# RWKV-7 diagonal-block inverse: forward substitution by columns in place of rows

## The chip, the core and the metric

The kernel runs on one core of a Trainium2 chip. The metric is device time in microseconds (us) of one execution. It was run three times before the change; the median is 3178.09 us. Engine names in the rows: PE is TensorE (PEld its weight loads), DVE is VectorE, ACT is ScalarE, POOL is GpSimd, SP is SyncE, which here only issues DMAs. A name with a q (SPq, ACTq) is the engine's queue of DMA issues, waits and the like.

## The reference, cut to what matters

Two layers of a streaming-encoder trunk are computed on 1024 tokens of width 1024. Layer 0 has RWKV-7 time mixing beside a Mamba-2 scan; then come cross-attention and an MLP; layer 1 has an mLSTM in place of the pair. The change is in the RWKV-7 part, whose core is this recurrence over time:

```python
def rwkv7_scan(r, w, k, v, a, b):
    def step(S, inp):
        r_t, w_t, k_t, v_t, a_t, b_t = inp
        sa = jnp.einsum('bhvk,bhk->bhv', S, a_t)
        S = S * w_t[:, :, None, :] + sa[..., None] * b_t[:, :, None, :] + v_t[..., None] * k_t[:, :, None, :]
        return S, jnp.einsum('bhvk,bhk->bhv', S, r_t)
    ...
```

The kernel computes it in 16 chunks of 64 tokens for 8 heads. Inside a chunk the dependence of later tokens on earlier ones is a unit lower triangular system, so the kernel needs, for each chunk and head, the inverse T of I - A, where A is strictly triangular and 64 x 64. It inverts the two 32 x 32 diagonal blocks by forward substitution on VectorE and joins them with small matmuls later (lines 663 to 678).

## The kernel before, in words

The program is written as one main thread of large matmuls and many generators ("streams"). The planner keeps `self.pt`, an estimate of TensorE's time, which `mm` and `tr` raise with each matmul (lines 193 to 205). A generator that yields a number asks to be resumed when `pt` has grown by that number times `self.lag` (line 163; the lag is 1.8 in this stage, 3.0 from line 1073 on); one that yields a function waits for a condition. `tick` after each group of matmuls resumes what is due; `until` jumps `pt` forward when the main thread has nothing to do. The order of the trace is the priority; a scheduler then puts each engine's instructions into a fixed order. On the chip each engine runs its own in order.

Layer 0's mixer (`mixer0`, line 959) runs these parts:
- The main thread projects the normalised input with 26 weight tiles (`fm`, 48 matmuls of 128x512 each). Each weight tile is loaded on the ACT queue (line 231) and split in two parts, a cast on ACT (line 217) and a subtraction on VectorE (line 218).
- `rw_pair(p)` (line 495) prepares head pair p, for p 0 to 3. At its end four groups (lines 569 to 588, 2.5 planned us apart) multiply `bk` and `va`, mask the result into the tile `AB` (line 578) and store it on SP (line 579), and store transposed copies `tm` (lines 587, 588). Earlier it takes the product of line 564, and the tile `u` for `newton` (lines 487 to 493, 523).
- `rw_inverse(q)` (line 591) handles head pairs 2q and 2q+1, once both are prepared. It loads the diagonal blocks of all 16 chunks, 2 heads and 2 pairs into `As`, one 32 x 32 block per partition (128 of them), and makes `Ts` from the identity. Row i of `Ts` is then the sum over k of A[k, i] times row k, with `pr` holding the products. At the end `As` gets the transpose of `Ts` and twelve DMAs store both (line 626, eight on SP and four on ACT).
- `pr`, `AB` and `u` share one ring of two tiles of the pool `tmp` (tag "tmp", line 973).
- The last weight tiles are those of `z` (`mb_z`, line 818: a copy, a sigmoid of line 824 and a product on GpSimd of line 825) and, before the last of them, of dt (`mb_dt`, line 797: a chain of small operations over ACT and VectorE that ends in the scan of line 815).
- After the last projection the main thread waits for both inverses (line 1069), closes the pools of the stage, and goes on with the memory side of layer 1 (`memside`). The chunk loop (`rw_chunk`, line 630) waits for the inverses at line 652, loads T (lines 654, 655) and runs the recurrence; the Mamba windows (`mb_window`, line 828) load `a8` at line 845. Both are streams beside `memside`.

GpSimd runs the products of lines 548, 554, 788 and 825 during this stage.

Of the kernel before, what the change touches and what calls it, by code (L numbers as in the profile page):

```python
# [14 lines left out]
ALU = mybir.AluOpType  # L15

P = 128
# [38 lines left out]
class Trunk:  # L56
# [534 lines left out]
    def rw_inverse(self, q, pool, pt, S):  # L591


        nc = self.nc
        yield lambda: 0.0 if self.rw_done[0] >= 2 * q + 2 else None
        B = 32
        block = lambda s: self.ed.tile([P, B, B], F32, name=self.n(s), tag="xo") if q else pool.tile([P, B, B], F32, name=self.n(s), tag=s)
        As = block("As")
        for a in range(2):
            for j in range(2):  # L600
                src = S["ABK"][:, CH * j:CH * j + CH, 2 * q + a, j, :]
                r0 = 64 * a + 32 * j
                for b in range(2):
                    v = src[:, B * b:B * b + B, B * b:B * b + B]
                    self.ld1(As[r0 + 16 * b:r0 + 16 * b + 16], v)
        Ts = block("Ts")
        yield 9.0
        nc.gpsimd.memset(Ts[:], 0.0)
        nc.gpsimd.memset(Ts[:].rearrange("p i k -> p (i k)")[:, 0:B * B:B + 1], 1.0)
        for i in range(1, B):  # L610

            if i < 8 and i % 4 == 1 or i >= 8:
                pr = pt.tile([P, B, B], F32, name=self.n("pr"), tag="tmp")
            pv = pr[:, :i, :i]
            nc.vector.tensor_tensor(pv, Ts[:, :i, :i].rearrange("p k j -> p j k"), As[:, :i, i].unsqueeze(1).broadcast_to([P, i, i]), ALU.mult)  # L615
            nc.vector.tensor_reduce(Ts[:, i, :i], pv, mybir.AxisListType.X, ALU.add)  # L616
            if i >= 7 or i % 4 == 0:
                yield 0.4 + 0.0025 * i * i
        nc.vector.tensor_copy(As[:], Ts[:].rearrange("p i k -> p k i"))
        for n_, x in enumerate((Ts, As)):  # L620
            for a in range(2):
                for j in range(2):
                    r0 = 64 * a + 32 * j
                    for b in range(n_ + 1):
                        dst = S["T"][n_, :, CH * j + B * b:CH * j + B * b + B, 2 * q + a, B * b:B * b + B]
                        (nc.scalar if b else nc.sync).dma_start(dst, x[r0 + 16 * b:r0 + 16 * b + 16])
        self.inv_done[0] += 1
        self.inv_t = self.pt + 5.0
# [1220 lines left out]
```

## Time and profile before

| | |
|---|---|
| three runs | 3170.97, 3178.09, 3180.80 us; median 3178.09 |
| profiled execution | 3178.65 us, of which the span of the trace is 3176.9 us |
| mean granted TensorE clock | 0.969 of full speed |
| busy: TensorE / VectorE / ACT / GpSimd | 2957.1 / 1793.5 / 1316.6 / 621.2 us |
| line 615 (multiply), 62 instructions | 62.48 us of VectorE |
| line 616 (reduction), 62 instructions | 31.02 us of VectorE |
| first inverse | 333.95 us to about 452 us |
| second inverse | 472.45 us to about 533 us |

Times of a row are counted from the start of the span. A row of a timeline gives start, duration (for a merged row, of all of it), engine, line, operation, output from inputs, shapes, and in brackets how long the engine had been idle before and what released it. Busy times can overlap between engines; a matmul's end is modelled. Instructions of one engine can overlap a little.

### The profile page before, as it was taken

Reading aid. Unit: us, or ns where it says so; the run is one execution under the profiler, and the core shown is the slowest. Engines: PE = TensorE matmul, PEld = TensorE weight load, DVE = VectorE, ACT = ScalarE, POOL = GpSimd, SP = SyncE. Lnnn points to the kernel's source line nnn. Section 1 sums busy time; section 2 is a strip of 40 time slices with the busy share of each in tenths; the row PEclk is TensorE's granted clock in tenths of the full one; section 3 lists DMA queues with packets and bytes.
Section 4 is the critical chain, followed back from the end, with each engine's and each line's share of the span. In section 5 each row is a group of like instructions: output and inputs, shape, how many; then the busy total and the mean of one; then the engine's idle time right before and its main releaser. Section 6 shows DMA issues by size and latency. Waiting matters only on the chain.

```text
span 3176.9 us, 40016 instructions
## 1 busy us (share of the span) xinstructions
PE 2957.1 (93%) x15652; PEld 2394.3 (75%) x15652; DVE 1793.5 (56%) x2283; ACT 1316.6 (41%) x2096; POOL 621.2 (20%) x632
## 2 busy tenths in 40 slices
PE   8999997889889989998999999899999899989998
PEld 8777676867677867776788778777788677768877
DVE  7345788655653465664656732145644656646566
ACT  6546533434333343444443433133343444444433
POOL 1111121022221123333001110011221233330002
PEclk9999999979999989999999999999999999999999
DMA  7734466668552123445744543446331234457456
GB/s 262 262 93 124 121 165 167 211 223 273 177 180 99 67 91 128 138 137 205 257 157 159 177 146 99 123 128 227 114 113 67 80 134 141 136 193 259 144 163 221
DMA packets 274493, 505.21 MB, mean 159 GB/s; under 512 B 57328, under 2 KB 160176, under 8 KB 274304
## 3 DMA queue, kind: packets, MB, share of 16 engines
q1 hardware_dynamic: 220608, 317.50, 31.2%
q0 software_dynamic: 26144, 99.69, 8.8%
q10 hardware_dynamic: 27552, 85.47, 8.3%
q8 instruction: 123, 2.02, 0.3%
q14 instruction: 66, 0.54, 0.1%
HBM read 347.66 MB, written 154.89 MB: 158 GB/s over the span
## 4 chain that ended last, share of the span: by engine, by line
PE 66%; DVE 12%; DMA 11%; issue 4%; ACT 3%; SPq 1%; POOL 1%; DVEq 0%; ACTq 0%; POOLq 0%
PE pd L201 38%; PE pm L201 22%; PE ph L201 4%; DMA rw<-in_ff_dn_dram 3%; PE pm L205 3%; DVE wb L218 2%; DVE pr L615 2%; DMA ru<-scr 1%; DVE Ts L616 1%; DVE sx L218 1%; DMA scr<-mo 1%; DVE T L218 1%; DVE ce L786 1%; DMA yr<-scr 1%; DMA wr<-in_ev_w_out_dram 1%
## 5 line engine op out<-in xcount | busy, mean ns | idle before, releaser
L201 PE MATMUL pd<-xth,wb 128*128 128x512 f32 x1120 | 364.9, 401 | 11.1 <-DVE wb L218 10.9
L218 DVE TENSOR_TENSOR wb<-wr,wb 128x1024 fp32r<-128x1024 f32 (+1 forms) x148 | 180.9, 1228 | 273.1 <-ACT wb L217 272.6
L201 PE MATMUL pd<-w,sh 128*128 128x512 f32 x1024 | 324.5, 398 | 8.8 <-DVE y L341 5.6
L201 PEld LDWEIGHTS pd<-xth,wb 128*128 128x128 f32 x1120 | 210.9, 190 | 67.3 <-DVE wb L218 13.6
L201 PE MATMUL pd<-T,wb 128*128 128x512 f32 x1008 | 251.0, 395 | 11.3 <-DVE wb L218 5.8
L201 PEld LDWEIGHTS pd<-T,wb 128*128 128x128 f32 x1008 | 191.3, 190 | 55.1 <-DVE wb L218 6.7
L217 ACT ACTIVATE wb<-wr 128x1024 fp32r<-128x1024 f32 (+1 forms) x148 | 154.6, 1050 | 187.0 <-PE pm L201 116.3
L201 PEld LDWEIGHTS pd<-w,sh 128*128 128x128 f32 x1024 | 192.0, 190 | 51.5 <-ACT w L217 5.8
L201 PE MATMUL pd<-xtl,wb 128*128 128x512 f32 (+1 forms) x576 | 229.1, 399 | 0.0
L201 PE MATMUL pd<-xb,wb 128*128 128x512 f32 x768 | 194.3, 403 | 28.0 <-DVE ub L1564 20.4
L201 PE MATMUL pd<-w,sl 128*128 128x512 f32 x512 | 203.2, 397 | 0.0
L201 PEld LDWEIGHTS pd<-xb,wb 128*128 128x128 f32 x768 | 143.1, 190 | 73.4 <-DVE ub L1564 30.5
L201 PE MATMUL pm<-wb,xth 128*128 128x512 f32 x512 | 163.1, 399 | 0.5 <-DVE G L1213 0.5
L201 PE MATMUL pm<-wb,wb 128*128 128x512 f32 x672 | 157.1, 389 | 0.0
L201 PE MATMUL pm<-T,wb 128*128 128x512 f32 x528 | 140.4, 410 | 10.9 <-DVE T L218 5.2
L201 PEld LDWEIGHTS pm<-wb,wb 128*128 128x128 f32 x672 | 126.1, 188 | 26.1
L218 DVE TENSOR_TENSOR wb<-ws,wb 128x1024 fp32r<-128x1024 f32 x64 | 90.9, 1420 | 94.0 <-ACT wb L217 94.0
L201 PEld LDWEIGHTS pm<-T,wb 128*128 128x128 f32 x528 | 104.9, 200 | 37.3 <-DVE T L218 6.7
L217 ACT ACTIVATE wb<-ws 128x1024 fp32r<-128x1024 f32 x64 | 67.6, 1057 | 147.3 <-PE pd L201 122.4
L201 PEld LDWEIGHTS pd<-xtl,wb 128*128 128x128 f32 (+1 forms) x576 | 107.7, 187 | 25.8 <-issue 2.6
L201 PE MATMUL pd<-wb,wb 128*128 128x512 f32 x480 | 113.8, 394 | 5.1 <-DVE wb L218 5.1
L201 PE MATMUL pm<-sx,sx 128*128 128x512 f32 x384 | 96.3, 406 | 21.9 <-ACT sx L217 21.3
(436 smaller groups left out, 6309.4 us busy)
## 6 DMA issues: line engine op xcount, KB each, us to landing
scr<-ub POOLq DMA_DIRECT2D x32, 1792.0 KB, 8.6
ru<-scr SPq DMA_DIRECT2D x112, 512.0 KB
rw<-in_ff_dn_dram SPq DMA_DIRECT2D x82, 512.0 KB
scr<-xo POOLq DMA_DIRECT2D x39, 512.0 KB, 3.0
scr<-mo POOLq DMA_DIRECT2D x32, 512.0 KB, 5.6
xo<-scr SPq DMA_DIRECT2D x32, 512.0 KB
wr<-in_ff_upT_dram SPq DMA_DIRECT2D x32, 512.0 KB
wf<-in_ff_upT_dram SPq DMA_DIRECT2D x32, 512.0 KB
```

The lines of the kernel that those rows point to most:

```text
L201: self.nc.tensor.matmul(out, lhsT=lhsT, rhs=rhs, start=start, stop=stop, skip_group_check=on)
L205: self.nc.tensor.transpose(out, in_, self.ident if ident is None else ident)
L217: self.nc.scalar.activation(hi, src, AF.Copy)
L218: self.nc.vector.tensor_tensor(lo, src, hi.bitcast(F32), ALU.subtract)
L615: nc.vector.tensor_tensor(pv, Ts[:, :i, :i].rearrange("p k j -> p j k"), As[:, :i, i].unsqueeze(1).broadcast_to([P, i, i]), ALU.mult)
L616: nc.vector.tensor_reduce(Ts[:, i, :i], pv, mybir.AxisListType.X, ALU.add)
L786: nc.vector.scalar_tensor_tensor(e[:, d:], sg[:, :T - d], col(3 - d), e[:, d:], ALU.mult, ALU.add)
```

## The change

Row-wise substitution is replaced by column-wise substitution in the loop of `rw_inverse`. Once row k of `Ts` is final, its products with A[k, i] are added into all rows i below it: a multiplication over n x m elements and an addition of the same size in place, with n = 31 - k rows and m = k + 1 columns. The reduction is gone. The products lie contiguous at the head of `pr`. A `pr` tile is taken every eighth step. The stream yields after every second step, with a due time that grows with n x m.

```diff
-        for i in range(1, B):
-
-            if i < 8 and i % 4 == 1 or i >= 8:
+        for k in range(B - 1):
+
+            if k % 8 == 0:
                 pr = pt.tile([P, B, B], F32, name=self.n("pr"), tag="tmp")
-            pv = pr[:, :i, :i]
-            nc.vector.tensor_tensor(pv, Ts[:, :i, :i].rearrange("p k j -> p j k"), As[:, :i, i].unsqueeze(1).broadcast_to([P, i, i]), ALU.mult)
-            nc.vector.tensor_reduce(Ts[:, i, :i], pv, mybir.AxisListType.X, ALU.add)
-            if i >= 7 or i % 4 == 0:
-                yield 0.4 + 0.0025 * i * i
+            n, m = B - 1 - k, k + 1
+            pv = pr[:].rearrange("p i k -> p (i k)")[:, 0:n * m].rearrange("p (i j) -> p i j", j=m)
+            nc.vector.tensor_tensor(pv, As[:, k, m:].unsqueeze(2).broadcast_to([P, n, m]), Ts[:, k, :m].unsqueeze(1).broadcast_to([P, n, m]), ALU.mult)
+            nc.vector.tensor_tensor(Ts[:, m:, :m], Ts[:, m:, :m], pv, ALU.add)
+            if k % 2:
+                yield 0.4 + 0.004 * n * m
         nc.vector.tensor_copy(As[:], Ts[:].rearrange("p i k -> p k i"))
```

## Rows read from the trace of the kernel before

**Rows 1.** The page, chain that ended last: shares by engine, then by line.
```profile
PE 66%; DVE 12%; DMA 11%; issue 4%; ACT 3%; SPq 1%; POOL 1%; DVEq 0%; ACTq 0%; POOLq 0%
PE pd L201 38%; PE pm L201 22%; PE ph L201 4%; DMA rw<-in_ff_dn_dram 3%; PE pm L205 3%; DVE wb L218 2%; DVE pr L615 2%; DMA ru<-scr 1%; DVE Ts L616 1%; DVE sx L218 1%; DMA scr<-mo 1%; DVE T L218 1%; DVE ce L786 1%; DMA yr<-scr 1%; DMA wr<-in_ev_w_out_dram 1%
```
**Rows 2.** Stretches: length; PE, PEld, DVE, ACT, POOL busy; granted clock; DMA.
```profile
333.00:460.00 127.00, 115.48 (x599) 83.74 (x599) 106.05 (x121) 57.99 (x75) 22.95 (x16) 0.97 0.47 129
460.00:500.00 40.00, 38.43 (x184) 30.45 (x180) 28.78 (x50) 10.74 (x15) 10.27 (x5) 1.00 0.91 275
500.00:560.00 60.00, 40.42 (x206) 34.02 (x207) 43.75 (x35) 18.44 (x19) 6.18 (x4) 0.86 0.53 131
560.00:900.00 340.00, 299.04 (x3240) 252.84 (x3240) 199.24 (x377) 142.89 (x318) 69.92 (x85) 0.90 0.64 213
```
**Rows 3.** Timeline of PE, 388 to 565 us, rows with idle time before them.
```profile
427.74 1.06 PE L205 MATMUL pm<-ct,bk 64*128 64x64 f32 x8 [1.93 <-DVE xn L564]
...
441.51 0.73 PE L205 MATMUL pm<-ct,bk 64*128 64x64 f32 x8 [1.12 <-ACT tm L587]
453.21 0.46 PE L205 MATMUL pm<-ct,bk 64*128 64x64 f32 x4 [1.60 <-ACT tm L587]
501.54 0.50 PE L201 MATMUL pd<-xth,wb 128*128 128x512 f32 x1 [3.00 <-DVE wb L218]
516.29 1.15 PE L201 MATMUL pd<-xth,wb 128*128 128x512 f32 x2 [5.07 <-DVE wb L218]
534.09 0.58 PE L201 MATMUL ph<-mh,wb 128*128 128x256 f32 x1 [5.49 <-ACT zs L824]
...
559.43 0.38 PE L205 MATMUL pm<-ct,a 8*128 8x8 f32 x2 [7.07 <-DMA a<-scr]
```
**Rows 4.** Timeline of DVE: one step of either size, stretched ones, weight splits.
```profile
333.95 1.62 DVE L615 TENSOR_TENSOR pr<-Ts,As 128x1 f32<-128x1 f32 x1 [1.14 <-DMA As<-scr]
...
472.45 0.16 DVE L615 TENSOR_TENSOR pr<-Ts,As 128x1 f32<-128x1 f32 x1 [4.58 <-DMA As<-scr]
...
500.79 0.69 DVE L218 TENSOR_TENSOR wb<-wr,wb 128x512 fp32r<-128x512 f32 x1
...
504.02 3.42 DVE L615 TENSOR_TENSOR pr<-Ts,As 128x576 f32<-128x576 f32 x1
...
515.02 1.22 DVE L218 TENSOR_TENSOR wb<-wr,wb 128x1024 fp32r<-128x1024 f32 x1
...
527.73 1.86 DVE L615 TENSOR_TENSOR pr<-Ts,As 128x961 f32<-128x961 f32 x1
...
531.85 1.13 DVE L616 TENSOR_REDUCE Ts<-pr 128x31 f32<-128x961 f32 x1
```
**Rows 5.** Line 744: durations ns min/median/max, first and last start, shapes.
```profile
L744 DVE TENSOR_TENSOR yw<-yw,st x8: 681/691/693, 601.6 to 843.8; 128x512 f32<-128x512 f32 x8
```
**Rows 6.** Stretches, tile pr alone (lines 615, 616): length; DVE busy; clock; DMA.
```profile
390.00:452.00 62.00, 29.84 (x24) 1.00 0.46 130
472.00:534.00 62.00, 47.04 (x62) 0.94 0.54 171
```
**Rows 7.** Timeline of POOL: the product beside the multiply at 504.02.
```profile
503.99 2.37 POOL L825 TENSOR_TENSOR ze<-ze,zs 128x1024 f32<-128x1024 f32 x1 [0.77 <-ACT zs L824]
```
**Rows 8.** Timeline of ACT: the casts of the two late weight tiles.
```profile
492.50 0.64 ACT L217 ACTIVATE wb<-wr 128x512 fp32r<-128x512 f32 x1
...
503.79 1.06 ACT L217 ACTIVATE wb<-wr 128x1024 fp32r<-128x1024 f32 x1
```
**Rows 9.** Timelines of DVE and of SP's queue: dt scan, load of a.
```profile
534.82 4.20 DVE L815 TENSOR_TENSOR_SCAN ce<-rm,cs 8x1024 f32<-8x1024 f32 x1 [0.20 <-DMA scr<-ce]
...
551.04 1.84 SPq L845 DMA_DIRECT2D a<-scr  x1
```
**Rows 10.** Chain that ended last, in order of time: a store of AB.
```profile
324.85 4.69 DMA scr<-AB
```

## The prediction

> **What bounds the kernel now.** I read the chain of work that ended last first: TensorE holds 66% of it, and VectorE comes next with 12% [rows 1]; the two lines of the substitution stand in that list by name on the page. So VectorE can matter, but only in stages. The busy times by stretch show where: from 333 to 460 us, where the first inverse runs, VectorE is busy 106 of 127 us; from 500 to 560 us, where the second one ends, TensorE falls to 40.42 of 60 us, and its mean granted clock to 0.86 [rows 2]. Third, TensorE's idle times and what ended them [rows 3]: 3.00 and 5.07 us wait for the weight split of line 218 (VectorE), 5.49 us for the last sigmoid (ACT, line 824), 7.07 us for a small load; the earlier three (4.65 us in all) wait for VectorE's line 564 and for ACT's line 587. Fourth, VectorE's order of time [rows 4, 8]: the split that began at 500.79 had its ACT half done at 493.14 (492.50 + 0.64), the one at 515.02 at 504.85. For 8 and 10 us they stood behind steps 19 to 27 of the second substitution. What ends last in this stage is VectorE's queue, with TensorE (in order) behind it.
>
> **What is removed and added on VectorE.** Row by row, step i multiplies i x i elements and sums them by a reduction: the sum of i² for 1 to 31 is 10,416 elements in each of the two instructions. By columns, step k multiplies n x m and adds n x m, n = 31 - k, m = k + 1: the sum is 5,456, so 10,912 elements in two instructions against 20,832. Instructions stay 62 an inverse. Rates: the multiply reads both inputs at steps of 32 elements; 961 elements took 1.86 us, one element 0.16 [rows 4], so 1.77 ns an element. The reduction of 961 took 1.13 us; with the same start that is 1.01 ns. For the new multiply (one input repeated along the innermost index, the other contiguous) the nearest row is line 744, an addition with such a repeated input: 512 elements in 0.691 us [rows 5], so 1.04 ns; the contiguous 128x1024 of line 218 took 1.22 us [rows 4], the same rate. The bounds for the new pair are 1.04 and 1.77 ns; I take 1.04, since both new instructions walk contiguous rows and the repeated input has a row of its own. Only the first step's addition, with rows of one element, walks at a step of 32, and it has 31 elements.
>
> Old, undisturbed: 62 x 0.16 + 10,416 x (1.77 + 1.01) ns = 9.9 + 29.0 = 38.9 us an inverse. New: 9.9 + 10,912 x 1.04 ns = 9.9 + 11.3 = 21.2 us (29.2 at the other bound). The pauses between a step's dependent instructions are as many as before.
>
> **What GpSimd does to them.** The multiply at 504.02 took 3.42 us where its neighbours' rate gives 1.18, and GpSimd's line 825 ran from 503.99 for 2.37 us [rows 4, 7]. Of the 62 multiplies eight are stretched like this (the first at 333.95, the last at 504.02 [rows 4]). So the second inverse was busy 47.04 us [rows 6] and not 38.9: 8.1 us are such stretches. No reduction was stretched so, and the change puts two-input additions in the place of all 62. I still take what I find in the old one, cut to 5 us, since the new inverse lasts less long; bounds 0 and 8 and, if each addition that meets such a GpSimd instruction is held too, some 3 more (it would have met the next multiply anyway). Sum: 47 to 26 us, 21 us off VectorE in each inverse. The Trainium skill, "GPSIMD Engine Reference", section "Key points", says that GpSimd shares its SBUF interfaces with VectorE, with contention for VectorE instructions that have two SBUF inputs: it speaks against the additions and agrees with the row of 3.42 us; if it doubled the old loss of 8 us, the second inverse would be busy 37 us and save 10 in place of 21.
>
> The Trainium skill, "VectorE: DVE Perf Modes", section "Rules for kernel authors", calls the reduction "the slowest DVE op". Were the multiply no dearer than it, the old inverse would be 31.0 us and the saving undisturbed 10 in place of 18; here the reduction is the cheaper of the two by rows 4, and the measurement decides.
>
> **Where in the inverse it is saved.** Old costs grow with i², new ones are largest in the middle and equal at both ends. The first twelve steps get dearer: 24 x 0.16 + 650 x 2.78 ns = 5.6 us before, 24 x 0.16 + 1,846 x 2.08 ns = 7.7 us after. The last twelve fall from 3.8 + 7,946 x 2.78 ns = 25.9 to 7.7 us. Those last twelve are what stood before the two weight splits.
>
> **The order.** The planner is told 0.4 + 0.0025 i² at 26 places, 36.3 us, now 0.4 + 0.004 nm at 15 places, 16.9 us; with the lag of 1.8 these are 65 and 30 us of planned TensorE time. So the second inverse, which outlived the projections, is planned to end inside them. It issues twelve stores (eight SP, four ACT); they move from behind the dt scan and the last z into the projections, past the z stores on SP and the weight casts on ACT. They cost nothing while a projection's matmuls cover them; without that cover, up to 1.84 us an issue, as that of a [rows 9], 7 us for ACT's four. The chunk loop's first matmuls, which wait for the inverse's loads, may then stand in TensorE's order among the last projections. Nothing before shows such a wait; the nearest row is the 7.07 us for a load [rows 3], so it costs 0 to 7; I take 2, as matmuls are put late where their inputs are planned late. The pr tile is now taken 4 times an inverse in place of 26, each held for eight steps in the ring of two that AB and u also use; I take 0, and give its price below.
>
> **What of it reaches the end**, by TensorE's idle times:
> - 333 to 460 us: of the 4.65 us of waits [rows 3] I take 3. VectorE spends 29.84 us on the substitution between 390 and 452 [rows 6], after the change under 10; the head gets dearer, so not all.
> - 501 and 516 us: of 8.07 us 7, and 3 us of clock. The granted clock has two levels, 1.2 and 2.4 GHz; a mean of 0.86 over 60 us [rows 2] means some 17 us at the lower level, so at most 8 us of lost work, in this stretch behind idle times. It was 1.00 in the 40 us before.
> - 534 us: of 5.49 us 2. The last z's cast and sigmoid stand on ACT behind the dt chain, which waits for VectorE; two table loads remain.
> - 559 us: of 7.07 us 5. The load of a (issued 551.04) follows the dt scan on VectorE (534.82, 4.20 us) [rows 9], which comes some 15 us earlier, while TensorE arrives 12 to 15 us earlier.
> - against it the new wait, 2.
> Sum 3 + 10 + 2 + 5 - 2 = 18 us. What is late next: TensorE itself with the projections, then the loads of the chunk loop. From 560 to 900 us TensorE is busy 299 of 340 us [rows 2] and moves as a whole. The profiled execution took 3178.65 us (span 3176.9), 0.6 us over the median of 3178.09; 3178.65 - 18 = 3160.7, against the median 3160. Bounds of the sum: all waits and the clock away and no new wait, 4.65 + 8.07 + 8 + 5.49 + 7.07 = 33, with some 5 more from a reordered stage behind: 3140. Only half of 501 and 516 and the new wait in full: 4 + 0 + 0 - 7, about no gain.
>
> **Rivals.**
> (1) VectorE comes free and another wait takes the place: the dt chain over ACT with its table loads, SP's queue, or the chunk loads. For it: the waits at 534 and 559 us name ACT and a DMA, not VectorE [rows 3]. Against: the two at 501 and 516 name VectorE alone. The gain is then 2 to 8 us: 3170 to 3176, say 3173.
> (2) Slower: the ring of two. AB's slot is held from its two masks (128x512 like line 744's, 2 x 0.69 us [rows 5]) until its store has landed; one such store stands in the chain with 4.69 us [rows 10]. That is 6.1 us, against a planned 2.5 x 1.8 = 4.5 between groups. While one pr holds the other slot through eight steps, each group is 1.6 us late, eight groups of two pairs make 13 us; a u tile in the one free slot, for four instructions of 128x1024 at 1.22 us [rows 4] in each pair, adds 10, and the lower clock after such stops some 5. That is 28 us, and with 15 gained elsewhere 3192. It decides from the point at which groups have only one slot for their whole length. Against: the old form took slots 26 times and TensorE's waits name no slot; the first inverse becomes shorter.
> (3) It doesn't do what it says: the repeated input doesn't stream, and both instructions run at 1.77 ns. Then 8 us less are saved in each inverse, the waits of 501 and 516 shrink by half and the gain is about 8: 3170.
> (4) More than forecast: the chunk recurrence starts inside the projections and the stage behind loses waits too: 33 to 38 us, 3143.
>
> **Chances.** Forecast (10 to 30 us off) 0.62; (1) 0.16; (2) 0.12; (3) 0.04; (4) 0.06. A difference of 0.3%, 9.5 us, is about what a measurement of this kernel can tell from none. Faster: 0.62 + 0.06 = 0.68; the same: 0.16 + 0.04 = 0.20; slower 0.12. The range leaves out (2) and the edge of (1) and (4): 3140 to 3177.
>
> **What would show it.** The two lines' busy time per inverse near 26 us against 47; a middle step of 256 elements at 0.43 us for both instructions; last step short. TensorE's idle times for line 218 near 500 us gone, and the clock of that stretch near 1.00; the scan of line 815 some 15 us earlier; memory-side matmuls starting some 15 us before 534. Wrong would be: new idle times of TensorE for cT or cTT loads, or for AB slots (line 578) in the stretch from 333 to 460 us, or a stage from 560 to 900 us that grows by what was won before it.

## The result, and the profile after

The changed kernel took 3139.68 us, the median of 5 runs (3134.78 to 3144.98), against 3178.09 us before. The ratio is 0.9881 with a 95% interval of 0.9867 to 0.9895, so the change gains 38 us, or 1.2%. The forecast was 3160 us with a range of 3140 to 3177: the direction was right, the gain was twice as large, and the time lies just below the range.

The profiled execution after the change took 3139.83 us (span 3138.1 us). Line numbers from 613 on are higher by one than before: the multiply is L616, the addition L617.

First the stretches of the two inverses, VectorE's work on the tile pr alone (length; VectorE busy; granted clock; DMA), to set against rows 6:

```profile
338.00:418.00 80.00, 29.32 (x62) 0.96 0.45 123
458.00:500.00 42.00, 30.42 (x62) 1.00 0.68 224
```

The second inverse is busy 30.42 us where it was 47.04 [rows 6]. VectorE's timeline shows the middle step, one stretched addition and the dt scan:

```profile
483.17 0.42 DVE L616 TENSOR_TENSOR pr<-As,Ts 128x256 f32<-128x256 f32 x1
483.63 0.42 DVE L617 TENSOR_TENSOR Ts<-Ts,pr 128x256 f32<-128x256 f32 x1
...
491.40 3.15 DVE L617 TENSOR_TENSOR Ts<-Ts,pr 128x175 f32<-128x175 f32 x1
...
520.79 2.28 DVE L816 TENSOR_TENSOR_SCAN ce<-rm,cs 8x1024 f32<-8x1024 f32 x1 [0.94 <-DMA scr<-ce]
```

GpSimd's product that runs beside the stretched addition:

```profile
491.96 2.38 POOL L826 TENSOR_TENSOR ze<-ze,zs 128x1024 f32<-128x1024 f32 x1
```

TensorE's waits in the same stage, to set against rows 3:

```profile
420.82 3.78 PE L201 MATMUL pm<-xn,rkw 128*128 128x512 f32 x4 [3.56 <-POOL xn L554]
...
507.51 0.24 PE L201 MATMUL pm<-cT,cAB 32*32 32x32 f32 x2 [3.96 <-DMA cT<-scr]
525.42 0.48 PE L201 MATMUL ph<-mh,wb 128*128 128x256 f32 x1 [2.49 <-ACT zs L825]
```

The two waits for line 218 at 501 and 516 us are gone, and so is the one for the load of a at 559 us [rows 3]. Two waits are new. At 420 us TensorE waits 3.56 us for GpSimd's line 554; and before 507 us it waits 3.96 us for the load of cT: the first matmuls of the chunk loop now stand among the last projections. The wait for the last sigmoid has shrunk from 5.49 to 2.49 us.

The start of an execution differs by some us from run to run: the same instruction of line 490 begins at 321.50 us before and at 325.83 us after. All landmarks below are counted from that instruction, while the rows stand as the trace has them. The first matmul of the memory side (the first row after the last projection, 534.09 [rows 3]) comes 13.0 us earlier after the change. The first matmul of the cross-attention comes 37.9 us earlier. So 24.9 us of the gain arise between these two, in the stage that the prediction let "move as a whole". Stretches ahead of and within that stage, first of the kernel before, then of the kernel after (length; PE, PEld, DVE, ACT, POOL busy; granted clock; DMA):

```profile
452.40:534.10 81.70, 67.23 (x296) 51.43 (x296) 67.16 (x83) 26.17 (x33) 14.19 (x8) 0.93 0.64 184
534.10:942.40 408.30, 351.17 (x3521) 297.43 (x3521) 228.54 (x405) 164.31 (x353) 78.76 (x97) 0.91 0.66 213
```

```profile
456.70:525.40 68.70, 62.27 (x318) 49.23 (x316) 50.41 (x79) 24.06 (x26) 14.03 (x8) 0.98 0.66 194
525.40:908.80 383.40, 342.28 (x3464) 291.77 (x3465) 229.60 (x408) 165.94 (x354) 82.61 (x101) 0.94 0.67 224
```

TensorE's idle time in the stage behind fell from 57.1 (408.30 - 351.17) to 41.1 us, its busy time from 351.2 to 342.3 us, and its mean clock rose from 0.91 to 0.94. The account of the two profiled spans (3176.9 - 3138.1 = 38.8 us) is: -4.3 for the later start, +13.0 ahead of the memory side, +24.9 in the stage behind it, and 5.2 behind the cross-attention's start. That last part lies between -0.4 and 8.2 us in the thirteen changed kernels, for those with no gain elsewhere too, so it is not read as an effect. The page's chain of waits after the change (to set against rows 1) has VectorE at 10% in place of 12%:

```profile
PE 70%; DMA 11%; DVE 10%; ACT 3%; issue 3%; POOL 1%; SPq 1%; DVEq 0%; ACTq 0%; POOLq 0%
```

### The profile page after: what moved, and what is told of

It is laid out like the page before. It is cut to its first block, busy times and chain, and to the rows that moved or that the text cites. A ratio compares the mean times of both kernels' runs of the same rounds, so it can differ in the third digit from the quotient of the medians.

```text
span 3138.1 us, 40034 instructions
## 1 busy us (share of the span) xinstructions
PE 2940.7 (94%) x15652; PEld 2385.3 (76%) x15652; DVE 1760.4 (56%) x2283; ACT 1316.5 (42%) x2096; POOL 627.8 (20%) x632
## 4 chain that ended last, share of the span: by engine, by line
PE 70%; DMA 11%; DVE 10%; ACT 3%; issue 3%; POOL 1%; SPq 1%; DVEq 0%; ACTq 0%; POOLq 0%
PE pd L201 40%; PE pm L201 23%; PE ph L201 5%; PE pm L205 3%; DMA rw<-in_ff_dn_dram 3%; DVE wb L218 2%; DMA aB<-scr 1%; DMA ru<-scr 1%; DVE sx L218 1%; DMA scr<-mo 1%; DVE Ts L617 1%; DVE T L218 1%; PE pq L201 1%; DVE pr L616 1%; DVE ub L1565 1%
## 5 line engine op out<-in xcount | busy, mean ns | idle before, releaser
L201 PE MATMUL pm<-sx,sx 128*128 128x512 f32 x384 | 95.0, 402 | 23.5 <-ACT sx L217 21.7
```

Source lines behind the costliest of these rows:

```text
L201: self.nc.tensor.matmul(out, lhsT=lhsT, rhs=rhs, start=start, stop=stop, skip_group_check=on)
```

## The experiments

The question was where the 25 us of the stage behind come from, and why the front gave 13 us. Three things were open: the plan (the yields and their due times), VectorE's real time, and the fixed order into which each engine's instructions are put when the kernel is built. "Start" below is the first matmul of the memory side, "stage" the time from there to the first matmul of the cross-attention, the start counted so that line 490 begins at 321.5 us in each:

| kernel | median us | ratio (95%) | start | stage |
|---|---|---|---|---|
| before | 3178.09 | 1 | 534.1 | 408.3 |
| after | 3139.68 | 0.9881 (0.9867 to 0.9895) | 521.1 | 383.4 |
| rows, new pace | 3172.73 | 1.0001 (0.9991 to 1.0011) | 529.2 | 412.2 |
| columns, old pace | 3131.01 | 0.9869 (0.9848 to 0.9889) | 520.8 | 380.0 |
| chunk loop behind projections | 3131.29 | 0.9870 (0.9849 to 0.9890) | 520.7 | 375.5 |
| loads early, matmuls late | 3125.73 | 0.9851 (0.9835 to 0.9866) | 520.6 | 371.2 |
| T held to the last projection | 3141.32 | 0.9879 (0.9864 to 0.9893) | 514.3 | 389.3 |
| VectorE busy behind the inverse | 3163.05 | 0.9948 (0.9931 to 0.9966) | 522.9 | 411.0 |
| rows first, columns second | 3158.94 | 0.9932 (0.9915 to 0.9949) | 530.8 | 387.1 |
| columns first, rows second | 3148.16 | 0.9898 (0.9883 to 0.9913) | 525.2 | 385.8 |
| rows shorter, same order | 3165.76 | 0.9960 (0.9946 to 0.9975) | 521.2 | 408.4 |
| columns longer, same order | 3152.91 | 0.9921 (0.9906 to 0.9936) | 531.4 | 386.7 |
| old pace and loads early | 3133.65 | 0.9866 (0.9849 to 0.9884) | 520.3 | 382.1 |
| one pr per inverse | 3142.46 | 0.9880 (0.9860 to 0.9901) | 519.3 | 389.7 |

Ratios are each against runs of the kernel before on the same chip; medians of different chips differ by some us.

**Is it the plan?** Two kernels cross the pace of the yields with the form of the loop. Columns with the old due times (edit of the kernel after):

```diff
-            if k % 2:
-                yield 0.4 + 0.004 * n * m
+            if m >= 7 or m % 4 == 0:
+                yield 0.4 + 0.0025 * m * m
```

> Columns on VectorE, but the stream pauses as the rows did: after steps with k + 1 = 4 and 7 to 31, with a due time of 0.4 + 0.0025 (k + 1)^2. So the second inverse is planned to outlive the projections, as before the change, while VectorE does the cheaper work. Theory A (head start: some 18 to 20 us of the 38 come from the chunk loop's start among the last projections, which is a matter of the plan): TensorE's waits near 500 and 516 us are gone, the stage from the first memory-side matmul to the first output projection is again about 289 us, and the time is 3160 (3153 to 3167). Theory B (VectorE's free time alone makes the gain, the stage behind follows from it): 3140 (3135 to 3147).

And rows with the new due times (edit of the kernel before):

```diff
-            if i >= 7 or i % 4 == 0:
-                yield 0.4 + 0.0025 * i * i
+            if i % 2 == 0:
+                yield 0.4 + 0.004 * (B - i) * i
```

> Rows on VectorE as before the change, but with the new pauses: after every second step, with a due time of 0.4 + 0.004 x (32 - i) x i. So the plan is that of the changed kernel, and VectorE does the dear work (47 us busy an inverse). Theory A: the chunk loop's matmuls stand among the last projections, but T comes some 35 us later than in the changed kernel; TensorE waits for the first cT load at about 507 us for 20 to 30 us in place of 4, part of it won back behind: 3160 (3150 to 3175). Theory B: VectorE is what decides, so 3178 (3170 to 3188).

Columns at the old pace gain 1.3%, at least as much as the change; rows at the new pace gain nothing. The shorter planned time of the inverse is not what gains. The gain belongs to the form of the loop.

**Is it the head start of the chunk loop?** After the change the first chunk matmuls stand inside the projections. Two kernels were meant to push them out; both are edits of the kernel after. One moves the loads and the matmuls of the whole loop behind the last projection:

```diff
-        yield lambda: self.inv_t if self.inv_done[0] == 2 else None
+        yield lambda: self.inv_t if self.inv_done[0] == 2 and self.dense[0] else None
...
+        self.dense = dense
```

> The changed kernel, but the chunk loop may load T and go on only once the projections are done and the pools of the stage are closed. VectorE's work and the inverse's end are as changed. Theory A: the 18 to 20 us behind the projections are lost: 3158 (3152 to 3164), and the stage from the first memory-side matmul to the first output projection is some 285 us in place of 269. Theory B: 3140 (3135 to 3147), perhaps 4 us better since the wait for cT at 507 us is gone.

The other leaves the loads where they are and moves only the matmuls:

```diff
         self.ld2(TT[:], S["T"][1, c])
+        if c < 2:
+            yield lambda: 0.0 if self.dense[0] else None
...
+        self.dense = dense
```

> The changed kernel, but the matmuls of chunks 0 and 1 are held until the projections are done, while their T loads are not. It parts theory A in two. A1 (matmuls moved into the projections are what counts, by filling TensorE's waits there and shortening the stage behind by their own length): 3150 to 3160, about as with both held. A2 (it is the loads that come before they are needed): 3138 to 3145, as the changed kernel. Theory B: 3140.

Both are as fast as the change or faster (3131.29 and 3125.73 us), but they don't answer the question as posed: the written order has the matmuls behind the projections, and in the trace the first of them still begins at 503.9 and 503.7 us, as after the change (503.2), because the scheduler brought them forward. What they show is another thing: VectorE's work on the inverses and the memory side's start (520.7 and 520.6 against 521.1 us) are those of the kernel after, and yet the stage behind lasts 375.5 and 371.2 in place of 383.4 us. Another order of the same work moves this stage by 12 us.

So the chunk loop was held back by data. The second inverse's last copy waits for a number that ACT makes (as zero) from the last projection's result:

```diff
+        if q:
+            yield lambda: 0.0 if self.zl is not None else None
+            nc.vector.tensor_tensor(Ts[:, 0, 0:1], Ts[:, 0, 0:1], self.zl[:], ALU.add)
         nc.vector.tensor_copy(As[:], Ts[:].rearrange("p i k -> p k i"))
...
```

> The changed kernel, with one true dependence added: the second inverse's result gets a zero added that is read from the last projection's output, so T leaves for memory some 24 us later (about 523 us) while VectorE does the substitution as early and as fast as before. The pace had no say (rows with the new pace ran as the kernel before, columns with the old pace as the changed one), so theory A in its first form is gone. Theory T1: what shortens the stage behind the projections (from the first memory-side matmul to the first of cross-attention, 408 us before, 383 changed) is that T arrives before that stage begins. Then the start of the memory side stays near 521 us, the stage goes back to 400 to 412 us, and the time is 3160 (3152 to 3170). Theory T2: VectorE's free queue at the end of the projections is all of it; the stage stays at 375 to 388 us: 3140 (3132 to 3147).

It took 3141.32 us: nothing is lost. TensorE's stretches and two of its waits in this kernel:

```profile
454.00:515.90 61.90, 58.44 (x258) 47.00 (x256) 49.92 (x78) 23.45 (x25) 14.33 (x8) 1.00 0.62 192
515.90:905.20 389.30, 341.30 (x3520) 292.27 (x3520) 225.22 (x405) 163.98 (x354) 79.41 (x97) 0.94 0.69 224
```

```profile
515.97 0.38 PE L201 MATMUL ph<-mh,wb 128*128 128x256 f32 x1 [3.53 <-ACT zl L831]
...
540.75 0.38 PE L205 MATMUL pm<-ct,a 8*128 8x8 f32 x2 [3.94 <-DMA a<-scr]
```

258 matmuls stand ahead of the start in place of 318 after the change, and the start comes 19.8 us earlier than before, not 13.0. The stage behind has 3520 matmuls, one fewer than before, and lasts 389.3 us, not 408.3. So, as far as this order shows, the chunk matmuls inside the projections neither gain nor cost: what they take in front (6.8 us of the start) they give back behind (5.9 us of the stage). Of the 19 us that the stage is still shorter, 9 are idle time (57.1 to 48.0) and 10 busy time of as many matmuls at a clock of 0.94 in place of 0.91.

**Which inverse?** The two inverses get different forms, in one kernel the first by rows and in the other the second (edits of the kernel after; the loop by rows is the old one unchanged):

```diff
+        if q == 0:
+            for i in range(1, B):
...
+        else:
+            for k in range(B - 1):
```

```diff
+        if q == 1:
+            for i in range(1, B):
...
+        else:
+            for k in range(B - 1):
```

> Only the second inverse by columns; the first by rows with its old pace and rings. The second one then begins near 472 us as before and ends near 508. The prediction on record gave the first inverse 3 us of the gain: then 3143 (3137 to 3150). If the second inverse's earlier begin (458 against 472 us) is due to the first one, T comes 14 us later than in the changed kernel, near the start of the memory side, and T1 gives 3152 (3145 to 3162).

> Only the first inverse by columns; the second by rows with its old pace. By the prediction on record 3 us of 38 or little more: 3172 (3165 to 3178). If the first inverse's early end brings the second one forward by 14 us, it ends near 518 us, T comes near 530, some 15 us ahead of the kernel before: T1 gives 3160 (3152 to 3168).

The expectation that the first inverse is worth only some 3 us missed in both kernels. The second inverse alone by columns gains 0.7% and the start comes 3.3 us earlier; the first alone gains 1.0% with 8.9 us. The two starts nearly add to the 13.0 of both, the times don't (0.7 and 1.0 against 1.2%): the stage behind lasts 387.1 and 385.8 us with either. One inverse by columns is enough for the shorter stage, whichever it is.

**VectorE kept busy behind the inverse.** Sixteen more instructions of 1024 elements follow the second inverse in the kernel after (they write pr, which nothing reads any more):

```diff
+        if q:
+            for _ in range(16):
+                nc.vector.tensor_tensor(pr[:], Ts[:], Ts[:], ALU.max)
```

> The changed kernel, but right after the second inverse VectorE does 16 more operations of 128x1024 (some 1.2 us each, 19.5 us; their results are not used). So T comes as early as in the changed kernel while VectorE has about the work it had before the change. T1: the waits for the weight split come back (8 to 10 us) and the memory side starts near 530 us, but the stage behind stays at 375 to 388 us: 3149 (3143 to 3157). T2: with VectorE's queue full again all is lost: 3170 (3162 to 3180).

It took 3163.05 us, with more than half of the gain gone. The start comes 1.8 us later than after the change; in the profiled execution, which at 3171.51 us was 8.5 us over this kernel's median, the stage behind lasts as long as in the kernel before:

```profile
523.80:934.80 411.00, 346.50 (x3465) 295.16 (x3465) 233.87 (x412) 165.68 (x354) 87.50 (x101) 0.91 0.64 208
```

This looked like VectorE's queue delaying the stage behind. But the added instructions also change the order that is derived when the kernel is built, so real time and order were still not separated.

**Real time against order.** Two kernels separate them. In both, the instructions of all five engines stand in exactly the order of the kernel they come from; only VectorE's durations differ. In the kernel before, the multiply reads contiguous rows (so that what is computed is not the inverse):

```diff
-            nc.vector.tensor_tensor(pv, Ts[:, :i, :i].rearrange("p k j -> p j k"), As[:, :i, i].unsqueeze(1).broadcast_to([P, i, i]), ALU.mult)
+            nc.vector.tensor_tensor(pv, Ts[:, :i, :i], As[:, i, :i].unsqueeze(1).broadcast_to([P, i, i]), ALU.mult)
```

> The kernel before, with one edit: the multiply of each row step reads its two inputs along contiguous rows (Ts[:, :i, :i] and As[:, i, :i]) in place of steps of 32 elements. The substitution then computes something else than the inverse, so its values aren't those of the reference; instructions, sizes, waits and the order of all five engines' instructions are exactly those of the kernel before. Only VectorE's time falls: by 10,416 x (1.77 - 1.04) ns = 7.6 us in each inverse, to some 39 of 47 us busy. Theory 'order' (the gain of the change comes from the other order in which the engines' instructions now stand, above all behind the memory side's start): nothing moves, ratio 1.000 within 0.002, the stage from the memory side's start to the first cross-attention matmul stays at 408 us. Theory 'queue' (the gain comes from VectorE being late less long in whatever order stands): 7.6 of the 17 us that the change takes off each inverse give about 0.45 of its gain, some 15 us, ratio 0.995, the memory side starts some 5 us earlier and the stage behind it gets shorter by some 10 us.

In the kernel after, the products stand transposed in pr:

```diff
-            pv = pr[:].rearrange("p i k -> p (i k)")[:, 0:n * m].rearrange("p (i j) -> p i j", j=m)
+            pv = pr[:, :m, :n].rearrange("p j i -> p i j")
```

> The kernel after, with one edit: the products of a step stand transposed in pr, so that the multiply writes and the addition reads at steps of 32 elements. The result and the order of all five engines' instructions are exactly those of the kernel after. VectorE gets 5,456 x 2 x (1.77 - 1.04) ns = 8 us longer in each inverse (29 to 30 us become 37 to 38), if a strided output costs what a strided input does; 4 us if only the read does. Theory 'order': the time stays that of the kernel after, ratio 0.988 within 0.002, stage behind 383 us. Theory 'queue': about half of the gain goes, ratio 0.993 to 0.994, memory side some 5 us later, stage behind some 10 us longer.

VectorE's busy time on pr in the two inverses of the shorter rows (to set against rows 6), and the stretches of that kernel:

```profile
333.00:447.50 114.50, 38.99 (x62) 0.97 0.46 131
466.00:521.00 55.00, 38.19 (x62) 0.94 0.60 193
```

```profile
521.70:930.10 408.40, 350.72 (x3521) 297.20 (x3521) 224.82 (x404) 164.00 (x353) 82.10 (x97) 0.91 0.66 213
```

The same of the longer columns:

```profile
335.00:419.00 84.00, 37.41 (x62) 0.96 0.44 123
456.00:507.00 51.00, 38.49 (x62) 0.94 0.59 188
```

```profile
534.20:920.90 386.70, 341.57 (x3463) 290.72 (x3464) 228.92 (x408) 165.63 (x354) 82.72 (x101) 0.93 0.66 221
```

The four kernels form a square. In the order of before, 8.9 us less on the second inverse (47.04 to 38.19) bring the start 12.9 us forward, and the stage behind stays at 408.4 us against 408.3. In the order of after, 8.1 us more (30.42 to 38.49) put the start 10.3 us back, and the stage stays nearly the same (386.7 against 383.4). At nearly equal VectorE time (38.19 and 38.49 us) the two orders take 3165.76 and 3152.91 us. So neither expectation held whole. VectorE's time moves the start and hardly touches the stage behind. The order does two things: it takes 21.7 us off the stage behind (408.4 to 386.7) and puts the start 10.2 us back (521.2 to 531.4). The steps add up to the change: -12.9 + 10.2 - 10.3 = -13.0 us at the start, 0.1 - 21.7 - 3.3 = -24.9 us in the stage. By the ratios (1, 0.9960, 0.9921, 0.9881) the gain has three about equal parts of 0.4%, each known to some 0.2%, 12 to 13 us each: VectorE's time from 47 to 38 us, the order, and VectorE's time from 38 to 30 us. The two middle kernels still differ in where within an inverse VectorE's time lies and in how often a pr tile is taken, so it is not shown that the 10.2 us at the start are the order's alone; the stage behind reacts little to VectorE's time in either order.

TensorE's waits in the shorter rows, for comparison with rows 3:

```profile
493.15 0.51 PE L201 MATMUL pd<-xth,wb 128*128 128x512 f32 x1 [0.73 <-DVE wb L218]
504.59 1.22 PE L201 MATMUL pd<-xth,wb 128*128 128x512 f32 x2 [3.33 <-DVE wb L218]
521.68 0.58 PE L201 MATMUL ph<-mh,wb 128*128 128x256 f32 x1 [3.47 <-ACT zs L824]
```

And in the longer columns:

```profile
502.30 0.79 PE L201 MATMUL pd<-xth,wb 128*128 128x512 f32 x1 [6.22 <-DVE wb L218]
515.12 0.31 PE L201 MATMUL pm<-cT,cAB 32*32 32x32 f32 x2 [2.72 <-DMA cT<-scr]
```

The wait for the weight split comes back as soon as the inverse is longer: this is the wait that the prediction named, shown from both sides.

**The best two together, and the ring.** The old pace and the late chunk matmuls in one kernel:

```diff
-            if k % 2:
-                yield 0.4 + 0.004 * n * m
+            if m >= 7 or m % 4 == 0:
+                yield 0.4 + 0.0025 * m * m
...
+        if c < 2:
+            yield lambda: 0.0 if self.dense[0] else None
...
+        self.dense = dense
```

> The kernel after with the old pace of yields (as in the run with columns at the old pace, 3131 us) and with the cT and cTT loads of the first two chunks early and their matmuls late (as in that run, 3126 us), both at once. If the two gains are of different kinds they add to some 3117 us, ratio 0.982; if both are only other orders of the same work, the time lies between 3120 and 3135 us, ratio 0.984 to 0.988.

3133.65 us: they don't add; each is another order of the same work. The fastest kernel stays the one with late chunk matmuls, 3125.73 us; its interval (0.9835 to 0.9866) ends just below that of the change.

Last, one pr tile for the whole inverse:

```diff
-            if k % 8 == 0:
+            if k == 0:
```

> The kernel after, with one edit: each inverse takes one pr tile for all its 31 steps in place of four for eight steps each. VectorE's instructions are the same; TensorE's order differs in 32 of its 14,112 matmuls. In the kernel after the first inverse stood still from 377.5 to 396.8 us between two pr tiles, and the second began right behind the first one's end and the next group's work. Theory 'ring harmless' (the change's four slots of the ring cost nothing that reaches the end): the first inverse ends some 15 us earlier, nothing else moves, ratio 0.988 within 0.002. Theory 'ring held the second inverse': the second inverse begins and ends up to 15 us earlier, the 3.96 us wait for the cT load goes, 3 to 6 us better, ratio 0.986 to 0.987. Theory 'ring of two, slower' (a pr that holds one slot for a whole inverse delays the groups of the RWKV heads, which then have one slot): up to 28 us worse, ratio up to 0.997, with idle times of TensorE for the masked products (line 578) between 340 and 420 us.

The first inverse, which stood still between 377.9 and 396.8 us for a new pr, ends 35.7 us earlier; the second begins 2.3 us earlier, and the time is that of the change (3142.46 us, ratio 0.988). The ring of two costs nothing that reaches the end, also with a slot held through 31 steps.

## Why the prediction was right and wrong

- **VectorE's work on an inverse: right, 3 to 4 us short.** Forecast were 26 us, measured 29.3 and 30.4; the middle step took 0.42 us for 256 elements (forecast 0.43). Both rates were right: in the shorter rows a contiguous multiply of 961 elements took 1.16 us, as 1.04 ns an element gives. The missing part is GpSimd's: eight instructions of the two inverses are stretched by some 2 us each, as many as before, and now three of them are additions (such as that of 491.40, 3.15 us). So 30.42 - 21.2, some 9 us, are lost to it; 5 were taken, with 11 as the bound (8 and 3). The shorter inverse did not meet fewer GpSimd instructions. The Trainium skill, "GPSIMD Engine Reference", section "Key points", names this contention for VectorE instructions with two SBUF inputs. The trace agrees for the additions; but with twice as many such instructions the loss stayed at 9 us and did not double to 16.
- **The front: 13 forecast, 13.0 measured, by luck, since two errors cancel.** The terms ahead of the memory side were 3 + 10 + 2 for VectorE's shorter time and -2 for the new order. In the square VectorE's time brings the start 12.9 us forward in the old order and 10.3 in the new one, 23.2 in all, and the change of order in between puts it 10.2 us back. On the first side, the 3 us of the first stretch were too few: in the kernel with shorter rows and the order of before, TensorE reaches the split of 501 us 8.9 us earlier (493.15 - 0.5 for its later start, against 501.54), of which 2.3 are the shorter wait there, so 6.6 were won before it. (The three waits that the prediction counted there leave out a fourth, 1.10 us for line 218 at 411.58 us.) The second inverse begins 18.8 us earlier, and 19.3 us earlier where the first alone goes by columns; that was not in the sum. In that kernel the start comes 8.9 us forward although the two waits for the split stay (4.95 and 4.50 us). On the other side, the new order puts 64 more matmuls ahead of the start (979 against 915, counted from line 490) behind a wait of 3.96 us for cT, where 2 were taken, and it has the new wait of 3.56 us at 420 us. Without the chunk matmuls the start is 19.8 us earlier, as the kernel with T held shows. The wait for the sigmoid gave 3.0 where 2 were taken. The clock ahead of the start rose as forecast, 0.93 to 0.98.
- **The wait of 559 us.** It went, as forecast with 5 us; but it lies in the stage behind, where it can't be told from the rest of the order's effect. In the order of before with less VectorE time it stays (the load of a still takes 6.07 us of TensorE's wait), so it went with the order and not, as argued, with the earlier scan. The same product of the next window, which had no wait before, waits 6.19 us for ACT's line 727 after the change (at 591.64 us).
- **The step that failed: "moves as a whole".** For a given order the sentence nearly holds: 408.3 and 408.4 us with 47 and 38 us of VectorE in the old order, 386.7 and 383.4 us with 38 and 30 us in the new one. But the change gives another order. The sum took 5 us in this stage, all of it for the wait of 559 us; for another order the prediction had allowed only with some 5 us in the bound. The stage got 24.9 us shorter, 21.7 of them by the order; net of what the order takes in front, the two kernels with equal VectorE time lie 12.9 us apart. The order was discussed only for the places next to the inverse (the stores, the first chunk matmuls); it reaches as far as the cross-attention.
- **The rivals.** Rival 1, another wait in place of VectorE's: no; the waits for cT and for the sigmoid together cost 6.5 us where 5.49 + 8.07 stood. Rival 2, the ring: no, by the kernel with one pr (its own sum, 3178 + 28 - 15, gives 3191 us and not 3192). Rival 3: no, 0.42 us a middle step. Rival 4 had the right time (3143 us), and half of its mechanism: the stage behind does lose waits. The other half, a recurrence that starts inside the projections, falls: with T held back the time is the same.

What stays open is which feature of an order makes the stage 408 or 383 us long. TensorE's idle time in it (length less busy time) parts the fourteen kernels: 57 to 65 us where it lasts 408 to 412 us, 31 to 48 in the others. No single wait makes this difference; the longest is 7.36 us in the kernel before and 13.09 us in the one after. Three orders that were derived with much VectorE work up to the end of the projections (before, rows at the new pace, VectorE busy behind the inverse) give 408 to 412 us; the others 371 to 390. In the shorter rows and the longer columns the real VectorE time is the same and the stage is not, so the order is the cause; which of its moves matters was not tried. Also open is a wait of 13.1 us just before the cross-attention, for VectorE's line 334, that some orders have (the kernel after and five of the experiments) and others not (the kernel before, all four that are faster than the one after, and three more):

```profile
904.87 1.94 PE L205 MATMUL pm<-ct,xn 128*128 128x128 f32 x8 [13.09 <-DVE xn L334]
```

## What to carry to other kernels

When a fixed order of instructions is derived from the program, a change to the cost of a few instructions is two changes: their time, which can be summed from the waits of the trace, and a new order, which can move stages far behind by as much as the first. Compare two kernels with the same order and different durations, and two with the same durations and different order, before explaining a gain by the waits it removed. And follow the earlier end of a stage into the start of the next one on the same engine: the first inverse, with few waits of its own, gave more than the second, beside which the waits stood.

## What the runs showed of the hardware

A multiply or an addition of 256 fp32 elements took 0.42 us with contiguous rows and 0.60 to 0.65 us when the multiply's output or one input of the addition stood at steps of 32 elements (the longer columns): for the output, too, the step costs about as much as for the inputs of the old multiply (0.63 us). A VectorE addition in place, which the prediction had only bounded, is held beside a GpSimd product about as long as a multiply is: 3.15 us where the same addition took 0.34 us in the first inverse. The same number of matmuls (3520 and 3521) was busy 341.3 us at a mean clock of 0.94 and 351.2 us at 0.91: of the two levels of the clock, the higher one held for a larger share where TensorE had idled less (48.0 us against 57.1), so that less idle time went with less busy time for the same work.
